# A two-layer transformer trunk: root of the sums without its own step, sums of exponentials in a ring, head scaling moved, and the last product in halves

## The chip, the cores and the metric

The kernel runs on one core of a Trainium2 chip. A core has TensorE (PE; PEld is its weight load), VectorE (DVE), ScalarE (ACT), GpSimd (POOL) and SyncE (SP), which only issues transfers here. The metric is the device time of one execution in microseconds. Matmuls write to PSUM, which has eight banks of 128x512 floats; the kernel gives four of them the tag "mm", two "s" and two "t".

## The reference, cut to what matters

The input is one sequence of 512 frames of width 1024, in float32. Two layers each compute, with `rms_norm(x, g) = x * rsqrt(mean(x*x) + EPS) * g`,

```python
y = mixer(rms_norm(x, attn_pre_g))
x = x + rms_norm(y, attn_post_g)
f = (silu(h @ w_gate) * (h @ w_up)) @ w_down      # h = rms_norm(x, ffn_pre_g)
x = x + rms_norm(f, ffn_post_g)
```

In layer 0 the mixer is a latent attention of 8 heads (q from a latent of 384, k and values from a latent of 256, a rotary part, a mask by chunks of 64 frames). In layer 1 it is an attention of 16 heads of width 64, with one key and value tensor projected from the residual stream, and a learned bias by distance. The feed-forward width is 2816.

## The kernel before, in words

Every matrix product is made three times: each operand is split into a high part (a cast on ScalarE, L144) and a low part (a subtraction on DVE, L145), and high·high, low·high and high·low are summed in PSUM (L361 to L363). The weights come in by SP's queue as `raw`, and their parts are called `whi` and `wlo`. The gate, up and down products of the feed-forward use seven block products in place of eight (`products`, L1524; `down`, L1280), for which DVE adds blocks of weights (L174).

Each engine has a queue of its own and executes it in order. The order in it is set when the program is built: a planner takes the instructions as they are written, with priorities that `first(n)` raises by n, and places them by its own estimate of when their inputs are ready. Thus a small edit can change the order at places that it doesn't mention.

**Attention** (`attention`, L546 and following) runs in slots, one per head and 128 queries. A slot computes the scores in a bank `sc` (L1069 to L1073 in layer 0, L1671 and L1672 in layer 1), their shifted values `p` and minimum `mn` on DVE (L527), exponentials with their row sums on ScalarE (L529), and two slots later the transposes `pt` (L541) and their split `pth`, `ptl`. When a head is complete, `pv` multiplies with the values (`b<-pth,va` in layer 0, L1679 and L1680 in layer 1). Between the slots, `weave` fills in the projections of later heads: q and k come out of `b` and are split into `qh`, `ql`, `kh`, `kl`; rotary parts are made by L971 to L973.

**The sums of exponentials** of a head stand in a tile `sums` of 128x32, memset to 1 on GpSimd for each. They are inverted on DVE (L1084, L1689), turned by a stream transpose (L503), written to memory by a transfer that GpSimd issues (`inv`) and read back, spread over the partitions, by two more (`rb`, L509). The head `of` is multiplied with `rb` (L1091 in layer 0, L1707 in layer 1), and then split into `oh` and `ol`. GpSimd's queue also holds the memsets of the bias tiles (L1603).

**Post-norms** sum squares of the projected bank by bank (`Sum.add`: Square on ScalarE, an addition on DVE, L439). `Sum.total` turns the sums on TensorE and reduces them on DVE (L452); `rstd` multiplies by 1/n and adds EPS on DVE (L463) and raises to the power −1/2 on GpSimd (L467); `spread` turns the result back over the partitions (L484). Between them TensorE works on.

**The last product.** `down` computes the 512x1024 result in quarters of two banks, each in seven steps; E6 is the last step, and its last group takes the weight tiles 3, 4 and 5. For each of its two banks (e is 0 or 1: the third and the fourth 128 rows) there follow: the last addition (L1347), the Square with its row sum (L1352), the gain (`yg`, L1467), the mean and EPS (`ssv`, L1389 and L1390), the root on GpSimd (L1393), and `plus_x` (L1491), which scales, adds the residual and sends the result out. `by_tokens`, called inside `products` of layer 1 three times for each pair of weight tiles, loads the residual stream back, turns it (L1196) and sends it to the output, to which the other rows' results are added.

Of the kernel before, what the change touches and what calls it, by code (L numbers as in the profile page):

```python
# [68 lines left out]
def trunk(ctx: ExitStack, tc: tile.TileContext, a, out):  # L69
# [353 lines left out]
    class Sum:  # L423


        def __init__(self, make=U):
            self.make, self.acc, self.begun = make, None, [False, False]

        def add(self, src, h=None):
# [4 lines left out]
            if not self.begun[h or 0]:  # L434
                ins = nc.scalar.activation(self.acc[:, c], src, AF.Square),
            else:
                q = self.make(name="sq")
                ins = (nc.scalar.activation(q[:, c], src, AF.Square),
                       V.tensor_tensor(self.acc[:, c], self.acc[:, c], q[:, c], op=OP.add))  # L439
            for i in ((0, 1) if h is None else (h,)):  # L440
                self.begun[i] = True
# [13 lines left out]
    def rstd(ss, n, eps=EPS):  # L455
        parts = ss if isinstance(ss, list) else [ss]
        m = sum(p.shape[1] for p in parts)
        v = small("v")[:, :m]
        w = m // len(parts)
        for i, p in enumerate(parts):  # L460
            o = v[:, i * w:(i + 1) * w]
            if eps is EPS:
                V.tensor_scalar(o, p, 1.0 / n, EPS, op0=OP.mult, op1=OP.add)  # L463
            else:
                V.scalar_tensor_tensor(o, p, 1.0 / n, eps[:, i * w:(i + 1) * w], op0=OP.mult, op1=OP.add)
        r = small("r")[:, :m]
        nc.gpsimd.tensor_tensor(r, v, mhalf[:, :m], op=OP.pow)  # L467
        return r

    def rstd_of_scaled(ss, n, r0):  # L470
# [4 lines left out]
        r = rstd(v, n)  # L475
# [19 lines left out]
    def sums_tile(i):  # L495
        t = pool[0].tile([P, 32], F32, tag="sums", name=f"sums_{i}", bufs=4)
        nc.gpsimd.memset(t, 1.0)
        return t

    def spread_dma(sums, i, m):  # L500

        t = pool[0].tile([P, 32], F32, tag="sumt", name=f"sumt_{i}", bufs=2)
        V.transpose(t, sums)  # L503
# [42 lines left out]
    def attention(n_heads, start, fill, first, units, after, pace=()):  # L546
# [18 lines left out]
        for i in range(slots + 3):  # L565
# [11 lines left out]
            if i >= 6 and i % NQT == 2:  # L577
                t = heads.pop((i - 6) // NQT)
                rest, far = t.pv(*t.pt)
                late.append((i + (NQT if far else 0), rest))  # L580
# [3 lines left out]
            if i % NQT == 3:  # L584
                scaled(i)
# [4 lines left out]
    class Post:  # L590
        def __init__(self, gain, make=U, eps=None, op=OP.add):

            self.gain, self.make, self.sum, self.y, self.r = gain, make, Sum(make), [], {}
            self.eps, self.op = eps, op

        def rstd(self, ss, h):
            return rstd(ss, D, EPS if self.eps is None else self.eps[:, 2 * h:2 * h + 2])
# [17 lines left out]
        def add_half(self, h, banks, rest, n1, n2, end=None):  # L615
# [7 lines left out]
            with behind(end and at):  # L623
                ss = self.sum.total(h, 200)
            with first(200):
                r = self.rstd(ss, h)
# [1200 lines left out]
```

## Time and profile before

| what | us |
|---|---|
| time, median of 3 runs (lowest, highest) | 1110.37 (1110.2, 1110.64) |
| the profiled execution's own time | 1110.27 |
| its span | 1108.5 |
| PE busy | 1094.3 |
| DVE busy | 936.8 |
| ACT busy | 678.3 |
| POOL busy | 91.7 |
| PE busy within 45 to 120 us (layer 0's attention) | 73.02 of 75.00 |
| PE busy within 560 to 700 us (layer 1's attention) | 138.21 of 140.00 |
| PE busy from 830 us to the end | 271.11 of 278.50 |

The granted clock of TensorE was 1.00 in each of these stretches. A row of a timeline gives the start, the duration, the engine, the line and operation with output and inputs, and in brackets how long the engine had been idle and whose end released it. Matmuls overlap: each lasts longer than the distance to the next start. A row of a list of waits gives the total, the number of times and the longest.

### The profile page before, as it was taken

To read this page: it belongs to the slowest core of one execution; us is meant where nothing else is said; L and a number is where in the kernel's file an instruction comes from. 1 tells how busy PE (TensorE), PEld (TensorE's weight loads), DVE (VectorE), ACT (ScalarE), POOL (GpSimd) and SP (SyncE) were. 2 spreads that over 40 slices of the span, in tenths; PEclk is the share of its full clock that TensorE was granted. 3 is DMA by queue.
4 is the path that set the end of the run, shared out by engine and by line. 5 is a ranking of instruction groups with operands and counts; after the bars stand their busy time and mean duration, and the time that the engine had idled before them with its cause. 6 is when DMAs were issued, how large, how long until landed. Compare 5 with 4: busy or idle time off the path is not lost.

```text
span 1108.5 us, 18978 instructions
## 1 busy us (share of the span) xinstructions
PE 1094.3 (99%) x6893; PEld 977.8 (88%) x6893; DVE 936.8 (85%) x1691; ACT 678.3 (61%) x1319; POOL 91.7 (8%) x158
## 2 busy tenths in 40 slices
PE   9999999999999999999999999999999999999997
PEld 6887889999999998888888788889999999998885
DVE  7778737999989989978868887758999999989977
ACT  6575737755555556668635676656755555556675
POOL 1211100000000001500000111000000000001402
PEclk9999999999999999999999999999999999999999
DMA  7443326323232357961556577635434444558913
GB/s 239 115 119 97 108 76 209 134 70 108 92 132 95 103 178 244 160 194 45 190 151 167 156 194 181 173 108 179 144 103 121 128 134 124 156 187 248 171 29 76
DMA packets 81421, 156.30 MB, mean 141 GB/s; under 512 B 26048, under 2 KB 27840, under 8 KB 81328
## 3 DMA queue, kind: packets, MB, share of 16 engines
q1 hardware_dynamic: 72448, 138.71, 40.5%
q0 software_dynamic: 8448, 15.95, 8.1%
q8 instruction: 54, 0.88, 0.3%
q10 hardware_dynamic: 432, 0.44, 0.1%
q14 instruction: 39, 0.32, 0.1%
HBM read 123.71 MB, written 10.88 MB: 121 GB/s over the span
## 4 chain that ended last, share of the span: by engine, by line
PE 85%; DVE 6%; DMA 4%; issue 2%; ACT 1%; SPq 1%; POOL 0%; DVEq 0%; POOLq 0%; ACTq 0%
PE al L1524 16%; PE b L361 10%; PE b L362 10%; PE b L363 10%; PE al L1280 8%; PE be L1524 8%; PE be L1280 5%; PE ga L1524 4%; PE de L1280 3%; PE ga L1280 3%; PE pt L541 2%; DVE wlo L145 2%; DVE raw L174 1%; DMA raw<-in_w_pair 1%; PE b L1680 1%
## 5 line engine op out<-in xcount | busy, mean ns | idle before, releaser
L144 ACT CAST whi<-raw 128x1024 fp32r<-128x1024 f32 (+3 forms) x224 | 225.0, 1006 | 200.6 <-PE al L1524 67.4
L145 DVE TENSOR_TENSOR wlo<-raw,whi 128x1024 fp32r<-128x1024 f32 (+3 forms) x224 | 260.1, 1164 | 43.3 <-ACT whi L144 41.9
L1524 PE MATMUL al<-th,whi 128*128 128x256 f32 x432 | 122.8, 285 | 0.2 <-DVE ut L1536 0.2
L1524 PE MATMUL al<-th,wlo 128*128 128x256 f32 x432 | 121.1, 281 | 0.3 <-DVE wlo L145 0.3
L1524 PE MATMUL al<-tl,whi 128*128 128x256 f32 x432 | 121.0, 280 | 0.0
L361 PE MATMUL b<-xh,whi 128*128 128x512 f32 (+1 forms) x298 | 114.8, 386 | 0.0
L363 PE MATMUL b<-xh,wlo 128*128 128x512 f32 (+1 forms) x298 | 110.0, 369 | 0.2 <-DVE wlo L145 0.2
L362 PE MATMUL b<-xl,whi 128*128 128x512 f32 (+1 forms) x298 | 109.8, 368 | 0.0
L174 DVE TENSOR_TENSOR raw<-raw,raw 128x1024 f32<-128x1024 f32 x72 | 86.9, 1218 | 1.1 <-DMA raw<-in_w_pair 0.8
L1524 PEld LDWEIGHTS al<-th,whi 128*128 128x128 f32 x432 | 81.3, 188 | 2.3 <-DVE ut L1536 0.6
L1524 PEld LDWEIGHTS al<-th,wlo 128*128 128x128 f32 x432 | 81.3, 188 | 0.6 <-DVE wlo L145 0.5
L1524 PEld LDWEIGHTS al<-tl,whi 128*128 128x128 f32 x432 | 81.4, 188 | 0.0
L529 ACT ACTIVATE p<-p,mn 128x128 f32<-128x128 f32 (+1 forms) x96 | 54.1, 563 | 37.6 <-DVE mn L527 37.2
L145 DVE TENSOR_TENSOR wlo<-wd,whi 128x512 fp32r<-128x512 f32 x86 | 56.4, 686 | 14.6 <-ACT whi L144 14.4
L145 DVE TENSOR_TENSOR ptl<-pt,pth 128x128 fp32r<-128x128 f32 (+1 forms) x96 | 46.4, 484 | 25.3 <-ACT pth L144 20.9
L363 PEld LDWEIGHTS b<-xh,wlo 128*128 128x128 f32 x298 | 56.2, 189 | 10.1 <-DVE wlo L145 0.6
L144 ACT CAST whi<-wd 128x512 fp32r<-128x512 f32 x86 | 49.8, 618 | 24.9 <-PE al L1280 10.7
L361 PEld LDWEIGHTS b<-xh,whi 128*128 128x128 f32 x298 | 56.5, 190 | 5.7
L362 PEld LDWEIGHTS b<-xl,whi 128*128 128x128 f32 x298 | 56.5, 190 | 5.5
L144 ACT CAST pth<-pt 128x128 fp32r<-128x128 f32 (+1 forms) x96 | 40.3, 421 | 28.3 <-PE pt L541 27.6
L245 POOL DMA_DIRECT2D wd<-in_w_down x22 | 19.5, 904 | 446.9 <-DVE raw L235 423.5
L1280 PE MATMUL al<-whi,pl 128*128 128x512 f32 x132 | 51.5, 390 | 0.0
(319 smaller groups left out, 3310.8 us busy)
## 6 DMA issues: line engine op xcount, KB each, us to landing
raw<-in_w_pair SPq DMA_DIRECT2D x72, 512.0 KB, 3.6
wd<-in_w_down SPq DMA_DIRECT2D x54, 256.0 KB, 5.9
raw<-in_w_o SPq DMA_DIRECT2D x16, 512.0 KB, 4.0
raw<-in_w_gu SPq DMA_DIRECT2D x16, 512.0 KB, 4.8
raw<-in_w_down SPq DMA_DIRECT2D x16, 512.0 KB, 4.3
raw<-in_w_qkb SPq DMA_DIRECT2D x16, 512.0 KB, 3.8
wd<-in_w_down POOLq DMA_DIRECT2D x22, 256.0 KB, 5.3
wd<-raw POOLq DMA_DIRECT2D x22, 256.0 KB, 4.2
```

The lines of the kernel that those rows point to most:

```text
L144: return (nc.scalar.copy(dst_hi, src), V.tensor_tensor(dst_lo, src, dst_hi.bitcast(F32), op=OP.subtract))
L145: V.tensor_tensor(dst_lo, src, dst_hi.bitcast(F32), op=OP.subtract))
L174: V.tensor_tensor(t, x, y, op=OP.add)
L245: nc.gpsimd.dma_start(p, self.src[0, e, :, c * S:c * S + S], accum_op=OP.add)
L361: nc.tensor.matmul(o, l[0], r[0], start=start, stop=False)
L362: nc.tensor.matmul(o, l[0], r[1], start=False, stop=False)
L363: last_mm[0] = nc.tensor.matmul(o, l[1], r[0], start=False, stop=stop)
L529: nc.scalar.activation(p[:, :n], p[:, :n], AF.Exp, bias=mn[:, :1], scale=-1.0, accum_out=self.sums[:, qt:qt + 1])
L541: nc.tensor.transpose(t[:, kt * P:(kt + 1) * P], p[:, kt * P:(kt + 1) * P], ident)
L1280: nc.tensor.matmul(to[e], l[c], r[d], start=j < 4 and k == 0 and n == 0, stop=k == NF // 2 - 1 and n == 2, skip_group_check=True)
L1524: nc.tensor.matmul(o, l[c], r[d], start=first_ and n == 0, stop=k == K2 - 1 and n == 2, skip_group_check=True)
L1680: nc.tensor.matmul(o[:, q_], vv, ptl[:, kt, q_], start=False, stop=kt == NQT - 1)
```

## The change

- `Sum` scales its squares by 1/1024 (the factor under the Square is 1024 to the power −1/2) and adds EPS/128 in its first addition, by one scalar_tensor_tensor. What `total` gives is then the mean plus EPS, and `rstd` is the power alone. Where the mean of fewer elements is wanted (the latents), the old way is kept, with the step written in `rstd_of_scaled`.
- The `sums` tiles become a ring of four (layer 0) and three (layer 1), memset once. The stream transpose of the sums has a priority of 60.
- A head's multiplication with `rb` and its split are written 7 slots behind its product with the values (for the last ones 5, or 1 as before), where it was 5. Whether one is due is asked in each slot, in layer 0 at its start and in layer 1 at its end; before, it was asked in layer 0 at the start of each, and in both layers at the end of every fourth.
- Two of the four value tiles of the first half take a bank of "s" instead of "mm".
- `by_tokens` isn't called in the first pair of `products`.
- In the last group of E6, bank e = 1 is computed in two halves of 256 columns, the first in its own bank, the second in a new one of tag "t", each with its own addition, Square, gain and `ssv` (`half`). What steps before the last group summed in the second half's columns is added to `y` ahead of it (`during`).

```diff
     class Sum:
-        def __init__(self, make=U):
-            self.make, self.acc, self.begun = make, None, [False, False]
+        def __init__(self, make=U, mean=True):
+            self.make, self.acc, self.begun, self.eps = make, None, [False, False], [mean, mean]
+            self.scale = D ** -0.5 if mean else 1.0
 ...
-            if not self.begun[h or 0]:
-                ins = nc.scalar.activation(self.acc[:, c], src, AF.Square),
+            t = self.acc[:, c]
+            both = (0, 1) if h is None else (h,)
+            if not self.begun[both[0]]:
+                ins = nc.scalar.activation(t, src, AF.Square, scale=self.scale),
             else:
                 q = self.make(name="sq")
-                ins = (nc.scalar.activation(q[:, c], src, AF.Square),
-                       V.tensor_tensor(self.acc[:, c], self.acc[:, c], q[:, c], op=OP.add))
+                ins = nc.scalar.activation(q[:, c], src, AF.Square, scale=self.scale),
+                if self.eps[both[0]]:
+                    ins += V.scalar_tensor_tensor(t, t, EPS / P, q[:, c], op0=OP.add, op1=OP.add),
+                    for i in both:
+                        self.eps[i] = False
+                else:
+                    ins += V.tensor_tensor(t, t, q[:, c], op=OP.add),
 ...
-    def rstd(ss, n, eps=EPS):
 ...
-                V.tensor_scalar(o, p, 1.0 / n, EPS, op0=OP.mult, op1=OP.add)
 ...
+    def rstd(v):
+        r = small("r")[:, :v.shape[1]]
+        nc.gpsimd.tensor_tensor(r, v, mhalf[:, :v.shape[1]], op=OP.pow)
         return r
 ...
-    def sums_tile(i):
-        t = pool[0].tile([P, 32], F32, tag="sums", name=f"sums_{i}", bufs=4)
-        nc.gpsimd.memset(t, 1.0)
-        return t
+    def sums_ring(n):
+        ring = [pool[0].tile([P, 32], F32, tag=f"sums{i}", name=name_("sums"), bufs=1) for i in range(n)]
+        for t in ring:
+            nc.gpsimd.memset(t, 1.0)
+        return ring
 ...
-        V.transpose(t, sums)
+        with first(60):
+            V.transpose(t, sums)
 ...
-                late.append((i + (NQT if far else 0), rest))
+                late.append((i + far, rest))
 ...
-            if i % NQT == 3:
+            if after:
                 scaled(i)
 ...
-            b = bank()
+            b = bank() if c or tt % 3 else bank("s")
 ...
-            return rest, far
+            return rest, (6 if h < H_A - 3 else 4) if far else 0
 ...
+                end = group[-1] == Down.TILES - 1
                 for e in range(2):
-                    for i, w, p in got:
 ...
+                    for o, cols in post.parts(j, e, to[e]) if end else ((to[e], ALL),):
+                        fresh = o is not to[e]
+                        for i, w, p in got:
 ...
+                        if cols is not ALL:
+                            post.half(o, cols)
+                        elif end:
+                            post.one(j, e, o)
 ...
+            if j == Down.E6 and i == 2:
+                t, c = self.y[0][3], HALF[1]
+                V.tensor_tensor(t[:, c], t[:, c], banks[1][:, c], op=OP.add)
 ...
+        def half(self, b, c):
+            t, v, q = self.y[0][3], self.v[:, 3:4], HALF.index(c)
+            with first(200):
+                V.tensor_tensor(t[:, c], t[:, c], b[:, c], op=OP.add)
+                sq = U(name="sq")
+                nc.scalar.activation(sq[:, c], t[:, c], AF.Square, accum_out=self.ends[:, q:q + 1])
+                if not q:
+                    self.yg = U(name="yg")
+                    V.scalar_tensor_tensor(v, self.ss[1][:, 3:4], 1.0 / D, self.eps[:, 3:4], op0=OP.mult, op1=OP.add)
+                V.tensor_tensor(self.yg[:, c], t[:, c], self.g[0][:, c], op=OP.mult)
+                self.summed = V.scalar_tensor_tensor(v, self.ends[:, q:q + 1], 1.0 / D, v, op0=OP.mult, op1=OP.add)
+                if q:
+                    self.y[0][3] = self.yg
+                    self.r[3] = small("r")[:, :1]
+                    nc.gpsimd.tensor_tensor(self.r[3], v, mhalf[:, :1], op=OP.pow)
 ...
                 if i == 2:
                     self.plus_x(1, 2, nc.sync)
+                    self.plus_x(0, 2, nc.scalar)
 ...
             with tc.issue_after(self.summed.ins):
-                self.plus_x(0, 2, nc.scalar)
                 self.plus_x(1, 3, nc.sync)
                 self.plus_x(0, 3, nc.scalar, nc.sync)
 ...
-                if aside is not None and j in (1, 3, 5):
+                if aside is not None and p and j in (1, 3, 5):
                     next(aside, None)
```

**How the order moves.** First, the post-norm of layer 1's attention, DVE's queue; `ss` is the reduced sum that the root needs, `wlo` the low part of a weight. Before:

```order
L452 TENSOR_REDUCE ss_8861<-tot_8858 128x2
L145 TENSOR_TENSOR wlo_9134<-raw_9049,whi_9133 128x1024
L463 TENSOR_SCALAR v_8863<-ss_8861 128x2
L439 TENSOR_TENSOR acc_8698<-acc_8698,sq_8893 128x256
L649 TENSOR_TENSOR y_8696<-y_8696,bc_8888 128x256
```

Now:

```order
L145 TENSOR_TENSOR wlo_9061<-raw_8923,whi_9060 128x1024
L460 TENSOR_REDUCE ss_8831<-tot_8828 128x2
L145 TENSOR_TENSOR wlo_9100<-raw_9017,whi_9099 128x1024
L447 TENSOR_TENSOR acc_8668<-acc_8668,sq_8861 128x256
L650 TENSOR_TENSOR y_8666<-y_8666,bc_8856 128x256
```

The step `v` behind the weight's part is gone; the reduction keeps its place.

Second, layer 0's attention where the fourth head's transposes are split, ScalarE's queue (`whi` is the cast of a weight, `qh` and `kh` those of q and k). Before:

```order
L144 CAST pth_1235<-pt_1320 128x4x128
L144 CAST qh_1241<-b_1170 128x512
L144 CAST whi_1551<-raw_1311 128x1024
L144 CAST kh_1243<-b_1247 128x512
L144 CAST qh_1327<-b_1288 128x512
```

Now:

```order
L144 CAST pth_1231<-pt_1314 128x4x128
L144 CAST whi_1536<-raw_1300 128x1024
L144 CAST qh_1237<-b_1161 128x512
L144 CAST kh_1239<-b_1243 128x512
L144 CAST qh_1321<-b_1277 128x512
```

The weight's cast has moved ahead of q's. On DVE its low part has moved ahead of `ql` in the same way, and on PE the first score matmul that reads `kh` has moved ahead of the product with the values.

Third, the end of DVE's queue. `be` are the banks of the last step, `last` the new one, `r` a root from GpSimd. Before:

```order
L1347 TENSOR_TENSOR y_12641<-y_12641,be_11914 128x512
L1467 TENSOR_TENSOR yg_12918<-y_12641,g_11944 128x512
L1390 SCALAR_TENSOR_TENSOR ssv_11909<-ss_1_11907,ssv_11909 128x1
L1491 SCALAR_TENSOR_TENSOR yg_12889<-yg_12889,r_12922,xt_12487 128x512
L1347 TENSOR_TENSOR y_12652<-y_12652,be_11915 128x512
L1467 TENSOR_TENSOR yg_12944<-y_12652,g_11944 128x512
L1390 SCALAR_TENSOR_TENSOR ssv_11909<-ss_1_11907,ssv_11909 128x1
L1491 SCALAR_TENSOR_TENSOR yg_12918<-yg_12918,r_12922,xt_12486 128x512
L1491 SCALAR_TENSOR_TENSOR yg_12894<-yg_12894,r_12948,xt_12491 128x512
```

Now:

```order
L1356 TENSOR_TENSOR y_12606<-y_12606,be_11879 128x512
L1482 TENSOR_TENSOR y_12617<-y_12617,be_11880 128x256
L1506 TENSOR_TENSOR yg_12884<-y_12606,g_11909 128x512
L1402 SCALAR_TENSOR_TENSOR ssv_11873<-ss_1_11871,ssv_11873 128x1
L1488 TENSOR_TENSOR yg_12913<-y_12617,g_11909 128x256
L1529 SCALAR_TENSOR_TENSOR yg_12854<-yg_12854,r_12888,xt_12452 128x512
L1529 SCALAR_TENSOR_TENSOR yg_12884<-yg_12884,r_12888,xt_12451 128x512
L1489 SCALAR_TENSOR_TENSOR ssv_11873<-ends,ssv_11873 128x1
L1482 TENSOR_TENSOR y_12617<-y_12617,last_12894 128x256
L1488 TENSOR_TENSOR yg_12913<-y_12617,g_11909 128x256
L1489 SCALAR_TENSOR_TENSOR ssv_11873<-ends,ssv_11873 128x1
L1529 SCALAR_TENSOR_TENSOR yg_12859<-yg_12859,r_12937,xt_12456 128x512
```

Both steps that scale the third row block now stand ahead of the last addition; before, one of them stood ahead of it and one behind. On PE, nine 256-column matmuls of `be_11880` now stand between the last but two and the last but one matmul of `be_11879`.

84 lines of the change are left out of this document (42 added, 42 removed).

## The prediction

> **What bounds the kernel now.** I read the page first: the busy times, and the chain of work that ended last.
>
> ```profile
> span 1108.5 us, 18978 instructions
> PE 1094.3 (99%) x6893; PEld 977.8 (88%) x6893; DVE 936.8 (85%) x1691; ACT 678.3 (61%) x1319; POOL 91.7 (8%) x158
> PE 85%; DVE 6%; DMA 4%; issue 2%; ACT 1%; SPq 1%; POOL 0%; DVEq 0%; POOLq 0%; ACTq 0%
> ```
>
> TensorE is busy in 1094.3 of 1108.5 us, and the chain is on it for 85%. No edit removes a matmul, so the time can change in two ways only: by the moments at which TensorE stands still, and by what follows its last matmul. The profiled execution took 1110.27 us, so 1.77 us lie around the span; the median of the runs is 1110.37, which is 0.10 above it. The list of TensorE's waits, next, is short. Its two largest rows:
>
> ```profile
> PE b L1680 <- DVE ptl L145: 1.5, 1, 1.5
> PE bc L484 <- POOL r L467: 0.9, 1, 0.9
> ```
>
> Then I went through the timeline of each wait, as below. The most that the change can win is some 5 us of 1110, so every term is a few tenths. From a gap between two starts I take off the pitch at which matmuls follow each other when nothing waits: 0.12 us with 256 columns (760.93 and 761.05 below), 0.23 with 512 (1100.51 and 1100.73 in the tail's rows).
>
> **The reciprocal root without its own step (L463).** The end of layer 1's attention projection, the timeline of DVE, GpSimd and PE, and one row of the same place in layer 0:
>
> ```profile
> 759.51 0.42 DVE L452 TENSOR_REDUCE ss<-tot 128x2 f32<-128x256 f32 x1
> 759.85 1.21 DVE L145 TENSOR_TENSOR wlo<-raw,whi 128x1024 fp32r<-128x1024 f32 x1
> 760.98 0.16 DVE L463 TENSOR_SCALAR v<-ss 128x2 f32<-128x2 f32 x1
> 761.29 0.90 POOL L467 TENSOR_TENSOR r<-v,mhalf 128x2 f32<-128x2 f32 x1 [51.56 <-ACT sq L438]
> 760.93 0.28 PE L361 MATMUL b<-oh,wh 128*128 128x256 f32 x1
> 761.05 0.28 PE L362 MATMUL b<-ol,wh 128*128 128x256 f32 x1
> 762.24 0.43 PE L484 MATMUL bc<-ident,r 128*128 128x128 f32 x2 [0.92 <-POOL r L467]
> 183.03 0.43 PE L484 MATMUL bc<-ident,r 128*128 128x128 f32 x2
> ```
>
> The step itself lasts 0.16 us; it costs more because a weight's low part (L145, 1.21) stands between the reduction and it. Without the step GpSimd reads the reduction, done at 759.93. It started 0.15 after its input was ready (761.29 against 761.14), so now at 760.08; 0.90 later is 760.98, and the spreading matmul starts 0.05 after that (762.24 against 762.19), at 761.03. TensorE gets there 0.24 earlier than before, since the order has it two matmuls of 0.12 sooner: at 761.17 − 0.24 = 760.93. The wait falls from 1.07 to 0.10: **−1.0 us**. In layer 0 the same weight step stands in the same place, and the gap was about 0.3: **−0.3**. The gain of EPS and mean in the sums is paid with one scalar_tensor_tensor where a tensor_tensor stood, under a tenth of a microsecond on DVE, hidden by matmuls. Bounds of both together: −1.4, and nothing, if another input is last.
>
> **Sums turned earlier, ring of tiles.** The first pair of heads in layer 1:
>
> ```profile
> 608.31 0.20 DVE L503 STREAM_TRANSPOSE sumt<-sums 128x32 f32<-128x32 f32 x1
> 611.52 0.14 POOL L1603 MEMSET bias<- 64x64 f32 x1 [1.58 <-DMA bias<-in_rel]
> 612.30 1.09 POOL L509 DMA_DIRECT2D rb<-inv  x2 [0.64 <-PE pt L541]
> 617.46 0.69 DVE L1707 TENSOR_TENSOR of<-of,rb 128x512 f32<-128x512 f32 x1 [1.73 <-DMA rb<-inv]
> 619.21 0.55 DVE L145 TENSOR_TENSOR ptl<-pt,pth 128x384 fp32r<-128x384 f32 x1
> 620.75 0.50 PE L1680 MATMUL b<-ptl,vb 128*128 128x512 f32 x1 [1.50 <-DVE ptl L145]
> ```
>
> DVE waits 1.73 us for the reciprocals that travel through memory, ptl comes late, and TensorE stands 1.5 (1.65 by the starts). In the new order the transpose stands three rows sooner on DVE, some 0.8 us. But GpSimd's queue still holds the bias memset, which waits for its own load until 611.52, ahead of the second transfer: that one can start at about 611.7 instead of 612.30, so 0.6 is likely, and a transfer that starts ahead of its neighbours may also land faster: half of the remaining 1.05 on top. **−1.1** (0 to −1.65). The multiplication keeps its place among DVE's rows; only the split of the scaled head moves, and nothing reads it soon. The other pairs, and the first layer:
>
> ```profile
> 692.02 0.49 PE L1679 MATMUL b<-pth,vb 128*128 128x512 f32 x1 [0.24 <-ACT pth L144]
> 74.63 0.20 DVE L503 STREAM_TRANSPOSE sumt<-sums 128x32 f32<-128x32 f32 x1
> 82.83 0.69 DVE L1091 TENSOR_TENSOR of<-of,rb 128x512 f32<-128x512 f32 x1 [1.05 <-DMA rb<-inv]
> 86.66 0.50 PE L362 MATMUL b<-ptl,va 128*128 128x512 f32 x1 [0.59 <-DVE ptl L145]
> 97.63 0.50 PE L361 MATMUL b<-ckh,whi 128*128 128x512 f32 x1 [0.22 <-DVE ra L971]
> 105.04 0.63 PE L541 MATMUL pt<-ident,p 128*128 128x128 f32 x4
> 105.70 0.59 ACT L144 CAST pth<-pt 128x512 fp32r<-128x512 f32 x1 [0.54 <-PE pt L541]
> 106.19 0.59 ACT L144 CAST qh<-b 128x512 fp32r<-128x512 f32 x1
> 106.86 1.04 ACT L144 CAST whi<-raw 128x1024 fp32r<-128x1024 f32 x1
> 106.93 0.68 DVE L145 TENSOR_TENSOR ql<-b,qh 128x512 fp32r<-128x512 f32 x1
> 107.67 0.51 PE L361 MATMUL b<-pth,va 128*128 128x512 f32 x1 [0.61 <-DVE ql L145]
> ```
>
> At 692.02 DVE had been late by an earlier wait of the same kind; transpose and sums are a row earlier: **−0.4** (0 to −0.5). In layer 0 the first head's sums are turned right behind their reciprocal, over 3 us before 74.63, so the 1.05 us at 82.83 goes, and with it the stand at 86.66 (starts 85.67 and 86.66, less 0.23): **−0.75**. Scaling 7 slots behind instead of 5 takes the split `ol` (some 0.68, like `ql` at 106.93) out of DVE's way ahead of the rotary steps, and the matmul at 97.63 finds its bank free: its 0.22 and the slower start behind it, **−0.4**.
>
> **The price of the new order in layer 0.** Behind the fourth transpose at 105.04, ScalarE had cast q, then the weight; now the weight is first, and on DVE its low part stands ahead of `ql`. Count from the transposes' start t. ScalarE's first cast begins at t + 0.66 and the next 0.49 later (105.70, 106.19); the weight's cast ends at t + 2.2, q and k at t + 2.7 and t + 3.2. DVE's low part of the weight (1.13 from 759.85 to 760.98 above) then ends at t + 3.35, `ql` at t + 4.0. Before, `ql` was done at 107.61, t + 2.57, and TensorE was there at t + 1.85. The new order has the first score matmul, which needs k, only four matmuls of 512 behind the transposes, at t + 1.3, and the product with the values two short ones later. That product needs the bank that `ql` empties, so it starts at about t + 4.1: a stand of some 2.6 instead of 0.75. **+1.9**, between 0 (the cast of the weight gets done ahead of the transposes) and +2.4. Layer 0's attention thus gives −0.75 − 0.4 + 1.9 = **+0.75**. The value tiles that now take their banks from the scores' pair change no wait that I found: nothing, and up to ±0.3.
>
> **Products.** With the by-tokens work out of pair 0, its transposes stand in later pairs:
>
> ```profile
> 820.69 0.70 DVE L1196 STREAM_TRANSPOSE xt<-x 128x512 f32<-128x512 f32 x1
> 823.70 0.38 PE L1524 MATMUL al<-th,wlo 128*128 128x256 f32 x1 [0.33 <-DVE wlo L145]
> ```
>
> 0.70 us less ahead of the weight's low part covers the wait: **−0.4** (0 to −0.5). The later pairs already carried one such transpose each without a wait this long.
>
> **The tail.** The end of the last group on all engines:
>
> ```profile
> 1100.51 0.39 PE L1280 MATMUL be<-wlo,ph 128*128 128x512 f32 x1
> 1100.73 0.39 PE L1280 MATMUL be<-whi,pl 128*128 128x512 f32 x1
> 1101.16 0.69 DVE L1347 TENSOR_TENSOR y<-y,be 128x512 f32<-128x512 f32 x1 [0.36 <-PE be L1280]
> 1101.88 0.63 ACT L1352 ACTIVATE sq<-y 128x512 f32<-128x512 f32 x1 [2.72 <-DVE y L1347]
> 1102.64 0.16 DVE L1390 SCALAR_TENSOR_TENSOR ssv<-ss,ssv 128x1 f32<-128x1 f32 x1
> 1102.88 1.00 POOL L1393 TENSOR_TENSOR r<-ssv,mhalf 128x1 f32<-128x1 f32 x1 [2.87 <-DVE ssv L1390]
> 1103.91 1.54 DVE L1491 SCALAR_TENSOR_TENSOR yg<-yg,r,xt 128x512 f32<-128x512 f32 x3 [0.45 <-POOL r L1393]
> 1099.44 0.57 POOL L1393 TENSOR_TENSOR r<-ssv,mhalf 128x1 f32<-128x1 f32 x1 [3.43 <-DVE ssv L1390]
> ```
>
> Thirty matmuls of 256 columns take 3.5 us where fifteen of 512 took 3.4: +0.1, and TensorE ends at about 1101.2 as before. What was meant is plain: the last add and square have 256 columns, 0.42 instead of 0.69 (the reduction above has that size) and some 0.2 less on ScalarE: −0.5. But DVE's order puts two `plus_x` steps of the third row block, which wait for GpSimd's root, **ahead** of the last half's add. Nine matmuls of the other half now run before the first bank is done, so that is done 1.0 later, at 1098.7; then follow on DVE an add (0.7), a half add (0.4), a gain (0.65), the sum `ssv` at about 1100.5. GpSimd starts 0.24 later and takes 0.57 to 1.00 (both rows above): 1101.3 to 1101.75. Two `plus_x` and a small sum bring DVE to 1102.8 to 1103.3, long after TensorE has ended. Only then come the half add (0.4), the square (0.55), the sum (0.15), the wait for GpSimd again (0.65 to 1.1) and the last three steps (1.54): DVE ends at 1106.25 to 1107.1 instead of 1105.45, so +0.8 to +1.65: **+1.2**; −0.5 is kept as the other bound. The Trainium skill (PSUM — Partial Sum Buffer, Engine vs sequencer instructions) says that VectorE's queue is strictly first in, first out; by that rule the half add can't pass the two steps, and the trace agrees: DVE's 1101.16 to 1103.91 run in the order written.
>
> **Sum.** −1.0 − 0.3 − 1.1 − 0.4 + 0.75 − 0.4 + 1.2 = −1.25. The profiled execution would take 1110.27 − 1.25 = 1109.02; with the 0.10 that the median lies above, 1109.1.
>
> **The rivals.** *A, the tail as meant*: GpSimd's first root comes so early that the two `plus_x` steps are done when TensorE ends. Then −0.5 stands for +1.2, and the result is 1107.4. For it: GpSimd took only 0.57 the last time but one. Against it: even with that, `ssv` at 1100.5 gives 1101.3, and 1.5 us of steps follow. The Trainium skill (Perfetto Trace Analysis, Optimizing Scalar/DVE Operations) says that where Vector isn't saturated but causes bubbles, breaking up instructions may complete the work sooner; by that rule the result is this rival's. No row before the change shows a half. *B, the early turn wins nothing*: the second transfer is held by its neighbours, not by the transpose; then the 1.1, 0.4 and 0.75 are lost, 1111.4. For it: GpSimd's memset, and that DVE had its reciprocals only 5 us after 612.30; against it: the head at 82.83 has 3 us to spare. *C, slower*: a weight cast ahead of q and k also decides in the next two heads of layer 0, where the order again puts one before k; each costs 1.9, 3.8 together, 1112.9. It decides where k is asked for less than about 3.2 us after the transposes. Against it: other heads give TensorE value products between. *D*: both the tail and the stand at 105 cost nothing: 1109.1 − 1.7 − 1.9 = 1105.5.
>
> **Chances.** Forecast 0.48, its own range 1107.8 to 1110.4; A 0.22, B 0.17, C 0.08, D 0.05. A measurement of this kernel tells a change from none at about 0.2%, 2.2 us: faster is below 1108.15, slower above 1112.6. Faster: all of A and D and a quarter of the forecast, 0.39. Slower: C, 0.08. Within: 0.53. The range goes from 1106.8, which leaves out D and the better part of A, to 1111.4, which takes in B.
>
> **What would show it.** Right: GpSimd's root starts directly behind the reduction near 760, with no TensorE wait over 0.2 there; DVE's wait for `rb` in the first pair of layer 1 falls below 1.2, and that of layer 0 is gone; a TensorE stand of 2 us or more near 105; the last 256-column add runs over a microsecond after TensorE's last matmul. Wrong: DVE idle at that add until TensorE ends, which is A; TensorE's sum of waits in layer 0's attention lower by over a microsecond, which leads to D; or waits for `kh` in several heads, C.

## The result, and the profile after

The changed kernel takes 1118.69 us (median of 4 runs, 1116.1 to 1119.83), the kernel before, run beside it, 1110.44 (1110.2 to 1110.64): a ratio of 1.0071, interval 1.0051 to 1.0091. It is slower by some 8 us; 1109.1 was forecast, with 1111.4 as the upper end. The profiled execution took 1117.65 us, 7.4 more than the one before. The head of its page, and the largest rows of TensorE's waits (total, times, longest; the 1.2 us of the warm-up at the start, in both kernels, left out):

```profile
span 1115.9 us, 18985 instructions
PE 1096.5 (98%) x6908; PEld 980.7 (88%) x6908; DVE 938.9 (84%) x1687; ACT 678.1 (61%) x1321; POOL 92.2 (8%) x149
PE b L1719 <- DVE ptl L145: 3.5, 4, 1.3
PE sc L1071 <- ACT kh L144: 2.4, 2, 1.9
PE b L361 <- DVE va L145: 1.5, 1, 1.5
PE bc L483 <- POOL r L465: 0.6, 1, 0.6
```

Two rows are new (`kh`, `va`), one has grown (`ptl`, 1.5 before), and one has shrunk by 0.3 instead of going (`bc`, 0.9 before). To place the loss I took, for each two neighbouring matmuls, the distance of their starts less the pitch of the first one's width (0.06, 0.118, 0.176 and 0.23 us for 128, 256, 384 and 512 columns, 0.11 for a transpose of 128), and summed it by stretches. This is what TensorE loses there, to waits and to a lower clock. Some small loss is everywhere. In microseconds, with five experiments that are told below (`only_late`, `late_h1`, `only_vals`, `only_rt` and `only_root`):

| stretch | before | before, again | changed | late alone | late, not head 0 | banks alone | turn alone | root alone |
|---|---|---|---|---|---|---|---|---|
| 0–45 | 2.8 | 2.7 | 2.0 | 4.0 | 3.1 | 3.8 | 3.6 | 3.0 |
| 45–70 | 1.1 | 1.1 | **4.2** | 1.0 | 1.1 | **4.3** | 1.1 | 1.1 |
| 70–95 | 2.0 | 1.7 | 1.0 | 1.9 | 1.4 | 1.4 | 1.2 | 1.7 |
| 95–125 | 3.8 | 3.8 | **6.8** | **5.6** | 3.7 | 3.6 | 4.0 | 3.8 |
| 125–235 | 2.0 | 1.9 | 1.5 | 2.0 | 1.5 | 2.0 | 1.6 | 1.0 |
| 235–560 | 1.9 | 2.1 | 1.8 | 0.8 | 1.8 | 2.3 | 2.0 | 1.5 |
| 560–705 | 5.5 | 8.0 | 7.7 | 9.7 | 6.4 | 4.6 | 9.2 | 8.2 |
| 705–760 | 1.5 | 1.6 | 1.5 | 2.0 | 1.3 | 1.5 | 1.5 | 1.4 |
| 760–835 | 1.9 | 2.1 | 0.9 | 1.8 | 1.8 | 1.9 | 1.8 | 1.4 |
| 835–end | 1.5 | 1.9 | 3.0 | 1.6 | 1.7 | 2.0 | 1.6 | 1.5 |

From the first column to the third this is +6.7; of the rest of the 7.4, 0.6 lies behind TensorE's last matmul (7.4 us to the span's end before, 7.9 now). The stretches that lost are 45–70, 95–125, 560–705 and the end.

**95 to 125 us.** The predicted stand is there. PE, ACT and DVE around it, then windows of two microseconds (length; busy times of PE, PEld, DVE, ACT and POOL with their instructions; granted clock, DMA share, GB/s):

```profile
107.69 1.05 ACT L144 CAST whi<-raw 128x1024 fp32r<-128x1024 f32 x1
109.12 0.59 ACT L144 CAST kh<-b 128x512 fp32r<-128x512 f32 x1
107.49 0.39 PE L363 MATMUL b<-ckh,wlo 128*128 128x512 f32 x1
109.76 0.68 PE L1071 MATMUL sc<-kh,qh 128*128 128x128 f32 x2 [1.88 <-ACT kh L144]
110.69 0.80 PE L361 MATMUL b<-pth,va 128*128 128x512 f32 x1 [0.24 <-DVE ql L145]
107.00:109.00 2.00, 0.88 (x4) 0.38 (x2) 1.55 (x4) 1.88 (x3) 0.73 (x1) 1.00 0.59 123
109.00:111.00 2.00, 0.99 (x3) 0.70 (x4) 2.00 (x3) 1.68 (x4) 0.63 (x2) 0.73 0.63 158
111.00:113.00 2.00, 2.00 (x8) 1.72 (x8) 1.42 (x3) 0.00 (x0) 0.42 (x1) 0.50 0.85 252
113.00:115.00 2.00, 2.00 (x9) 2.00 (x9) 1.28 (x5) 1.39 (x4) 0.00 (x0) 0.50 0.93 256
117.00:119.00 2.00, 2.00 (x14) 1.69 (x13) 0.60 (x2) 1.21 (x5) 0.00 (x0) 1.00 0.00 0
```

TensorE stands 2.04 us for `kh` (107.49 to 109.76, less 0.23) and then 0.64 for `ql`, 2.7 together, where the forecast had 2.6. What it did not have is the column of the clock: behind the stand it is 0.50 until about 116.7 us, with 8 or 9 matmuls in two microseconds where 14 run at 1.00. By starts, 106 to 111 us loses 3.2 (before: 1.8), and 111 to 118 loses 2.8 (before: 0.4).

**45 to 70 us.** DVE near 57 us, with the matmul that waits; the changed kernel, then the one before:

```profile
55.96 0.68 DVE L973 TENSOR_TENSOR ra<-b,sin 128x512 f32<-128x512 f32 x1
56.56 0.68 DVE L974 TENSOR_TENSOR rb<-b,cos 128x512 f32<-128x512 f32 x1
57.15 0.81 DVE L145 TENSOR_TENSOR wlo<-raw,whi 128x640 fp32r<-128x640 f32 x1
57.89 0.68 DVE L145 TENSOR_TENSOR va<-b,va 128x512 fp32r<-128x512 f32 x1
58.62 0.50 PE L361 MATMUL b<-whi,ckh 128*128 128x512 f32 x1 [1.50 <-DVE va L145]
```

```profile
55.27 0.82 DVE L145 TENSOR_TENSOR wlo<-raw,whi 128x640 fp32r<-128x640 f32 x1 [0.57 <-ACT whi L144]
56.76 0.68 DVE L145 TENSOR_TENSOR va<-b,va 128x512 fp32r<-128x512 f32 x1
57.36 0.68 DVE L971 TENSOR_TENSOR ra<-b,sin 128x512 f32<-128x512 f32 x1
57.49 0.50 PE L361 MATMUL b<-whi,ckh 128*128 128x512 f32 x1
```

The value product of a later token tile needs the bank that DVE's `va` empties. Before, `va` ran first; now two rotary products and a weight's low part, 2 us together, stand ahead of it. That order came with the banks, as the experiments show. By the starts this stand is 1.65 us (0.28 before); a second one of 0.71, in which the scores wait for `kh` at 66.71, is new too, and the rest of the 3.1 us lost here is in smaller pieces.

### The profile page after: what moved, and what is told of

It is laid out like the page before. It is cut to its first block, busy times and chain, and to the rows that moved or that the text cites. A ratio compares the mean times of both kernels' runs of the same rounds, so it can differ in the third digit from the quotient of the medians.

```text
span 1115.9 us, 18985 instructions
## 1 busy us (share of the span) xinstructions
PE 1096.5 (98%) x6908; PEld 980.7 (88%) x6908; DVE 938.9 (84%) x1687; ACT 678.1 (61%) x1321; POOL 92.2 (8%) x149
## 4 chain that ended last, share of the span: by engine, by line
PE 83%; DVE 7%; DMA 5%; issue 2%; ACT 1%; SPq 1%; POOL 1%; DVEq 0%; POOLq 0%; ACTq 0%
PE al L1562 17%; PE b L361 10%; PE b L362 9%; PE b L363 9%; PE be L1562 8%; PE al L1287 8%; PE be L1287 5%; PE ga L1562 4%; PE de L1287 3%; PE ga L1287 3%; PE pt L542 2%; DVE wlo L145 2%; PE b L1719 1%; DMA rb<-inv 1%; PE b L1718 1%
```

## The experiments

Each ratio is against the kernel before on the same chip, with its interval. First, two parts taken out of the changed kernel, each with its lines as they were.

```diff
-            return rest, (6 if h < H_A - 3 else 4) if far else 0
+            return rest, NQT if far else 0                     # no_late, and the same in layer 1
-            if after:
+            if i % NQT == 3:                                   # no_late
-            b = bank() if c or tt % 3 else bank("s")
+            b = bank()                                         # no_vals
```

> The changed kernel with one part undone: a head's scaling is written 5 slots behind its values again, in both layers. Theory 1 (the later scaling reorders layer 0's attention, and the stand of 2.7 us at 107 us also takes TensorE's clock to half for some 5 us): the stand falls under 1 us, the granted clock stays at 1.00 from 45 to 120 us, layer 1's waits for rb fall from 4.1 to about 3, and the time is 1111 to 1113. Rival 1 (the other parts cost it: the halves, the bank of the values, the by-tokens work): 1117 or more. Both leave the stand of 1.65 us at 57 us, since the value tiles' banks alone give that order too.

> The changed kernel with all value tiles in the banks mm again. Theory 1: DVE's order near 57 us stays as in the changed kernel, since the later scaling gives it too, so the stand of 1.65 us stays; time 1117.5 to 1119.5. Rival 2 (the banks taken from s make that wait): the stand goes, 1115.5 to 1117.

Without the later scaling 1.0045 (1.0029 to 1.0061), without the banks 1.0043 (1.0025 to 1.0061), against 1.0071. Each is worth some 3 us, a difference of two ratios that is itself uncertain by about 3 us; each part alone, below, costs 2.0 and 2.8 us. Without the scaling the clock stays at 1.00 from 45 to 120 us and the stand at 107 is 0.78; without the banks 45 to 70 loses 1.1, and the slow clock stays. Two expectations missed. `no_late` took 1116.25 us, between its two ranges, and layer 1's waits for `rb` rose from 4.1 to 5.3 us instead of falling to 3. And theory 1 of `no_vals` kept the stand near 57 us, since the later scaling would give that order too; its rival came true, the order comes with the banks alone, as the table's 45–70 row shows.

Then the later scaling alone on the kernel before, and a test of its second half: does a stand of this length halve the clock by itself? `gaps` computes nothing of the reference; it alternates 66 to 78 matmuls of 512 columns with stands of eight lengths, five times, with no transfers in between.

```diff
+        for k in LENGTHS:                       # DVE additions that the next matmul waits for
+            for j in range(m): nc.tensor.matmul(b[1] if j else b[0], h[:, :P], h, ...)
+            for j in range(k): nc.vector.tensor_tensor(y[:, :256], y[:, :256], b[1][:, :256], op=OP.add)
```

> The kernel before with one part added: the scaling 7 slots behind. Theory 1: the stands at 57 (1.5 us) and 107 us (2.5 us) with half the clock behind the second, and more waits for rb in layer 1; 1115 to 1119. Rival 1: 1111.5 or less.

> Only stretches of 66 to 78 matmuls of 512 columns, with stands of about 1.5 to 4.2 us between them, five times each length; nothing of the reference is computed. Theory 1 (a stand alone lowers the clock): behind stands shorter than some length between 2 and 3 us the matmuls start every 0.23 us as before, behind longer ones every 0.43 us for some 3 to 7 us. Rival 3 (the half clock comes from the transfers of 250 GB/s that run at that moment in the changed kernel): 0.23 us behind all of them.

The later scaling alone gives 1.0018 (1.0007 to 1.0030), 1113.51 us, between the ranges of the two expectations; it has the stand at 107 us and not the one at 57. In `gaps`, of stands of 1.12 and 1.58 us none is followed by slow matmuls (10 stands), of 2.04 three of 5, of 2.49 all 5, of 2.95 four of 5, of 3.40 and more all 14. The slow stretch costs 1.3 to 2.9 us, mostly 1.7. Windows of ten microseconds around a stand of 1.58, two of 2.04 and one of 2.49:

```profile
36.00:46.00 10.00, 8.58 (x38) 6.77 (x37) 1.84 (x5) 0.00 (x0) 0.00 (x0) 1.00 0.00 0
57.00:67.00 10.00, 8.12 (x29) 6.25 (x28) 2.26 (x6) 0.00 (x0) 0.00 (x0) 0.83 0.01 2
222.00:232.00 10.00, 8.12 (x36) 6.36 (x35) 2.26 (x6) 0.00 (x0) 0.00 (x0) 1.00 0.00 0
76.00:86.00 10.00, 7.67 (x27) 5.81 (x26) 2.68 (x7) 0.00 (x0) 0.00 (x0) 0.83 0.00 0
```

So transfers are not needed for it, and it begins between 1.6 and 2.5 us. What decides in between is where the stand falls. In `gaps` the granted clock changes only on a grid of 3.41 us (at 59.81, 63.23, 80.29, 83.70 us and so on), and behind a stand it is 0.50 for one or two whole steps of it, as in these two:

```profile
59.82:63.22 3.40, 3.40 (x9) 2.63 (x10) 0.42 (x2) 0.00 (x0) 0.00 (x0) 0.50 0.03 5
124.68:128.08 3.40, 3.40 (x10) 2.63 (x9) 0.00 (x0) 0.00 (x0) 0.00 (x0) 0.50 0.00 0
```

The 13 stands with at most 1.62 us in any one step are followed by no slow matmul, among them two of 2.04 and one of 2.95 that the border of a step divides; the 26 with 1.97 us or more in one step all are. In the kernels the border lies near 2 us as well: `no_late` has a stand of 2.06 us in layer 1, 2.03 of it in one step, without slow matmuls. The grid lies differently in each execution (the clock first rises 6.69 us into one profile of the kernel before and 5.41 into the other). So a given stand can cost the clock in one run and not in the next; the mean granted clock fits this, 0.994 to 0.995 in three of the changed kernel's four runs and 0.999 in the fastest (1116.1 us). The Trainium skill (TensorE: Matmul & The Clock Gate, Why this matters for your kernels) advises to leave no gap over about 3 us between bursts of matmuls. Here the measurement decides: the limit is lower, about 2 us within one step of the grid.

Next, what is left without the two parts; the kernel before again, for its profile; four small parts (root, ring, turn, by-tokens) alone; and the halves taken out.

> The changed kernel without the late scaling and without the values' new banks. Theory: these two cost some 3 us each and are all that made the changed kernel slower; what is left is the gain at the roots and turns (-1.8 us) and the tail (+0.6): ratio 0.999, between 0.998 and 1.001, the clock at 1.00 from 45 to 120 us, and about 1 us lost from 45 to 70. Rival: another part (the tail in halves, or the longer waits of layer 1) costs as much: 1.003 or over.

> The kernel before once more, to have its profile on the chip on which the other experiments ran. In layer 1 (560 to 705 us) the changed kernel and its first three variants lost 7.7 to 9.7 us on TensorE's start-to-start times, the kernel before 5.3 in its first profile. Theory: the change itself lengthens the waits there (layer 1's values, the place of the by-tokens product): this profile shows 5.3 +- 0.5 us again, and the three waits for the value tile ptl of a pair's second half stay at 2.9 us together. Rival: they vary from one execution or one chip to another: over 7 us here too. Ratio 1.000 in either case.

> The kernel before with four parts of the change alone: no separate root step, the early turn of the sums with its ring of tiles, the mean and epsilon made with the squares, and the products and by-tokens order; without the late scaling, the values' new banks and the last group in halves. Theory: the terms of the prediction that are left are -1.0 and -0.3 for the root step, -0.4 and -0.75 for the early turn (the first pair's -1.1 was not seen in the changed kernel), which with +0.6 for layer 1's longer waits is about -1.8 us, ratio 0.998. Rival: the waits won there come back behind the next one: ratio 1.000.

> The changed kernel with the last group whole, as before. Theory: the halves cost the 0.6 us by which the span's end moved away from TensorE's last matmul (8.0 us against 7.4): 0.6 us under the changed kernel, ratio 1.0065 to the one before. Rival: the halves help as they are meant to, and the longer tail of the one profile comes from elsewhere: ratio 1.008 or over.

Measured: no_late_vals 1.0021 (1.0011 to 1.0032), between its two expectations, so these two are not all; before_again 1.0002 (0.9993 to 1.0011), with 8.0 us lost in layer 1 against 5.5 in the first profile; keep4 1.0011 (1.0001 to 1.0021), a loss where 0.998 was expected; no_halves 1.0061 (1.0047 to 1.0075), which can't be told from the changed kernel's 1.0071. The rival on layer 1 holds in part: the same program loses 2.5 us more or less there. Its timeline and DVE's waits from 560 to 705 us show why:

```profile
607.94 1.23 DVE L309 TENSOR_TENSOR raw<-raw,gains 128x1024 f32<-128x1024 f32 x1 [1.51 <-DMA raw<-in_w_qkb]
DVE raw L309 <- DMA raw<-in_w_qkb: 10.0, 4, 3.4
DVE of L1707 <- DMA rb<-inv: 3.8, 4, 1.4
```

A weight that came in time in the first profile is awaited 1.5 us in this one, and the score tiles queue behind it on DVE (1.5 us more lost by TensorE near 610); the second pair's `rb`, not awaited in the first profile, is awaited 1.15 (1.1 lost near 640). A stretch of layer 1 must not be compared between two single profiles.

Then each small part alone, five rounds each:

```diff
+        with first(60):                          # only_rt, with the rings; turn_l1: first(0 if i < H_A else 60)
             V.transpose(t, sums)
-                if aside is not None and j in (1, 3, 5):
+                if aside is not None and p and j in (1, 3, 5):      # only_aside
```

`only_root` is the change's edit of `Sum` and `rstd`, `only_halves` its edit of the last group. `best1` is only_root with the rings and `first(60 if i < H_A else 0)`; `late_h1` is only_late with `6 if 0 < h < H_A - 3 else 4`.

> The kernel before with the root step alone (scale in the squares, epsilon in the adds). The four small parts together came out 1.2 us slower (ratio 1.0011, 1.0001 to 1.0021) though their profile shows the waits at the roots and at layer 0's sums shorter. Theory A: the root step wins what its waits show, 0.3 to 0.5 us near 183 and 1.0 near 761, and costs nothing elsewhere: ratio 0.9988. Theory B: what it wins is lost again in layer 1's start (560 to 705 us), whose waits for late weight transfers and value tiles took 5.5 us in one profile of the kernel before and 8.0 in another: 1.000, with over 7 us there.

> The kernel before with the turned sums alone (their priority and the ring of tiles). Theory A: 0.4 us are won from 70 to 95 us and nothing is lost: ratio 0.9997. Theory B: the earlier turn puts the pair's three small transfers ahead of other work in layer 1 and costs some 2 us there: 1.001 to 1.002, with over 7 us lost from 560 to 705 us.

> The kernel before with the by-tokens product moved past layer 1's first pair of products alone. Theory A: it costs nothing (I had forecast -0.4 us): ratio 0.9996 to 1.000. Theory B: this is the part that makes the four small ones slower, by waits for the up-projection's tile ut behind 835 us (0.5 us more there in the changed kernels): 1.0005 to 1.002.

> The kernel before with the last group in halves alone. Theory A: two applications of the factor stand ahead of the last half's add, the end moves 0.6 us away from TensorE's last matmul, and the halves' matmuls add 0.1: ratio 1.0005. Theory B: the halves are worth what they cost: 1.000. Theory C: they cost more than the tail shows, as the step from the four small parts (1.0011) to the kernel with the halves but without late scaling and banks (1.0021) would have it: 1.001.

> The kernel before with the ring of tiles and the priority of the turn in layer 1 alone. Theory A: the turned sums cost in layer 1: with the earlier turn VectorE's product by the spread sums stands one or two score groups earlier in its queue at the third pair and waits there for its transfer, and the three transfers meet more traffic (they landed 4.5 us after their issue with the earlier turn, 4.1 without): 1.0015 to 1.002, over 8.5 us lost from 560 to 705 us. Theory B: what only_rt showed was chance, or layer 0's: 1.000.

> The kernel before with the root step, the ring of tiles and the early turn in layer 0 alone. Theory A: the root step's gain (0.9989) and layer 0's wait of 0.4 to 0.5 us near 86 us add up: 0.9985, 1109.0 us, which would beat both kernels. Theory B: what the ring of tiles or layer 0's turn wins is lost again in layer 1, which waits for its transfers whatever comes before: 0.9995 or over.

> The kernel before with the later scaling for all heads but the first, whose scaling stays at 4 slots: with that ScalarE's queue at 107 us is as before (query and key casts ahead of the weight cast). Theory A: the stand at 107 us and the halved clock behind it are all that the later scaling costs: ratio 0.999 to 1.0003, the clock at 1.00 from 95 to 125 us and 3.8 us lost there. Theory B: it costs in layer 1 too (9.7 us were lost from 560 to 705 us with the later scaling alone, against 5.5 and 8.0 before): 1.001 or over.

| part alone | ratio | interval |
|---|---|---|
| root step | 0.9989 | 0.9979 to 0.9999 |
| turned sums, both layers | 1.0016 | 1.0004 to 1.0028 |
| the same, layer 1 alone | 1.0013 | 1.0002 to 1.0025 |
| root step and layer 0's turn | 0.9996 | 0.9986 to 1.0005 |
| by-tokens moved | 0.9997 | 0.9984 to 1.0010 |
| halves | 1.0001 | 0.9990 to 1.0011 |
| later scaling, all but the first head | 0.9998 | 0.9988 to 1.0008 |

The root step wins, by an interval that only just leaves out 1. The early turn loses, and in layer 1; layer 0's adds nothing to the root step that can be told. The later scaling costs nothing once the first head keeps its 4 slots: the clock stays at 1.00 from 95 to 125 us, and the new order at 107 was its whole price as far as this can be measured. Its windows from 95 to 125 us, of the scaling alone and without the first head:

```profile
95.00:125.00 30.00, 27.60 (x149) 23.75 (x148) 23.65 (x55) 18.75 (x46) 5.73 (x11) 0.94 0.40 116
95.00:125.00 30.00, 28.86 (x162) 24.07 (x161) 24.66 (x59) 20.65 (x49) 5.72 (x11) 1.00 0.47 135
```

Why the early turn loses: the timeline of only_rt at the first and the third pair, and then the third pair's product of the kernel before.

```profile
608.59 0.20 DVE L505 STREAM_TRANSPOSE sumt<-sums 128x32 f32<-128x32 f32 x1
612.44 1.09 POOL L511 DMA_DIRECT2D rb<-inv  x2 [0.89 <-DMA inv<-sumt]
618.37 0.69 DVE L1742 TENSOR_TENSOR of<-of,rb 128x512 f32<-128x512 f32 x1 [2.05 <-DMA rb<-inv]
658.40 0.69 DVE L1742 TENSOR_TENSOR of<-of,rb 128x512 f32<-128x512 f32 x1 [0.85 <-DMA rb<-inv]
659.01 0.68 DVE L145 TENSOR_TENSOR ptl<-pt,pth 128x512 fp32r<-128x512 f32 x1
659.75 0.50 PE L1715 MATMUL b<-ptl,vb 128*128 128x512 f32 x1 [0.64 <-DVE ptl L145]
```

```profile
655.29 0.69 DVE L145 TENSOR_TENSOR ptl<-pt,pth 128x512 fp32r<-128x512 f32 x1
656.48 0.69 DVE L1707 TENSOR_TENSOR of<-of,rb 128x512 f32<-128x512 f32 x1
```

At the first pair the turn still comes behind a weight for which DVE waits, so the transfers start no sooner, and land no sooner. At the third pair the planner, presumably because it now expects `rb` sooner, has put the product one score tile earlier: ahead of `ptl`. The transfer isn't there, and `ptl` waits behind it. TensorE loses 0.4 to 1.9 us at this place in all eight kernels with layer 1's early turn, and nothing that shows (over 0.15 us) in the eleven without it. Whether this is the whole of the part's 1.4 to 1.8 us is not shown, since the stretch varies by 2.5 us from one profile to the next.

Last, the banks alone, the bank "s" for the first token tile alone (`bank() if c or tt else bank("s")`), and the root step with late_h1, to which the runs pointed:

> The kernel before with the values' banks alone. Theory A: they cost what the windows of the kernels that have them show, 4.2 to 4.5 us lost from 45 to 70 us against 1.1: +3.2 us, ratio 1.0029. Theory B: as the turned sums did in part, the loss is made up by shorter waits further on: 1.001 or less, with 4.2 us still lost from 45 to 70 us.

> The kernel before with an s bank for the values of the first token tile alone, not for the first and the last. VectorE's queue near 57 us is then ra, rb, va, ra, va, wlo in place of ra, rb, wlo, va. Theory A: the stand of 1.65 us near 57 us comes from the weight's rest (1.2 us of VectorE) ahead of the first values: it falls to 0.5 us or less, 1 to 2 us are lost from 45 to 70 us, ratio 1.000 to 1.001. Theory B: it comes from the two rotary products or from the bank itself: the stand stays over 1 us, ratio 1.002 or over.

> The kernel before with the root step and the later scaling for all heads but the first. Theory A: the root step's 0.9989 and the later scaling's 0.9998 add up: 0.9987, which beats both kernels with an interval under 1. Theory B: the gain before layer 1 is lost again in the waits there, as it was with the root step and layer 0's turn together (0.9996): 0.9996 or over.

The banks alone cost 1.0025 (1.0015 to 1.0035), with 4.3 us lost from 45 to 70. `vals_0` comes out at 1.0039 (1.0025 to 1.0053): the weight's part is behind the values, yet a stand of 0.98 remains where 1.65 was, for the two rotary products, and another of 1.9 appears:

```profile
58.35 0.50 PE L361 MATMUL b<-whi,ckh 128*128 128x512 f32 x1 [0.82 <-DVE va L145]
```

The second is for `kh`, at 66.89, and the clock behind it is 0.50 from 68 to 70 us. So neither expectation covers it: both kinds of work ahead of `va` count, and both uses of the scores' bank that were tried reorder the stretch to its harm (5.2 us lost from 45 to 70 here). `best2` gives 0.9989 (0.9979 to 0.9998), as the root step does alone. Either is 0.1%, some 1.2 us, faster than the kernel before; the later scaling adds nothing that can be told.

## Why the prediction was wrong, step by step

Three steps failed: the banks' term, put at nothing, cost 3 us; the clock behind the new stand had no term and cost 2.4; and the turned sums, forecast to win 1.5 us in layer 1, lost 1.4 there (1.0013).

**Bound and method.** The bound "the most that the change can win is some 5 us" holds, but nothing in the sum bounded what it can lose. "The time can change in two ways only", by TensorE's stands and by the tail, left out a third: matmuls that run at half the clock. Between the two waits that the prediction calls the largest the list has a third, 1.2 us of the warm-up matmuls at the start, which is the same in both kernels.

**Root step, −1.0 and −0.3: its size was wrong in layer 1.** The root starts where the forecast had it, 0.15 us behind the reduction (765.78 + 0.42, 766.35), but takes 1.56 us instead of 0.90. The changed kernel:

```profile
765.78 0.42 DVE L460 TENSOR_REDUCE ss<-tot 128x2 f32<-128x256 f32 x1
766.12 1.22 DVE L145 TENSOR_TENSOR wlo<-raw,whi 128x1024 fp32r<-128x1024 f32 x1
766.35 1.56 POOL L465 TENSOR_TENSOR r<-ss,mhalf 128x2 f32<-128x2 f32 x1 [50.81 <-DVE ss L460]
767.97 0.43 PE L483 MATMUL bc<-ident,r 128*128 128x128 f32 x2 [0.64 <-POOL r L465]
```

The weight's part, which stood ahead of the root before, now runs beside it, and the root ends 0.57 after it (767.91 and 767.34), about what a root takes by itself. Layer 0 shows the same; before, with VectorE idle beside the root, and then changed:

```profile
182.26 0.72 POOL L467 TENSOR_TENSOR r<-v,mhalf 128x2 f32<-128x2 f32 x1 [52.35 <-DVE v L463]
```

```profile
185.65 1.61 POOL L465 TENSOR_TENSOR r<-ss,mhalf 128x2 f32<-128x2 f32 x1 [50.91 <-DVE ss L460]
```

So moving it ahead of that step saved its own wait, not the weight's. The Trainium skill (SBUF — State Buffer, SBUF: two separate sides) says that VectorE with two SBUF inputs and GpSimd share a pair of ports as an exclusive lock, and that the one who starts later waits for the whole instruction; the trace agrees, with 1.56 and 1.61 us against 0.72. The wait fell from 0.92 to 0.64, and layer 0's small gap went as said. The part as a whole still gave about 1.2 us (0.9989), near the forecast's 1.3; since these two rows account for only 0.6 of it, that agreement is in part luck.

**Turned sums, −1.1, −0.4 and −0.75: the sign was wrong in layer 1.** In the first pair the rows of `only_rt` fit rival B: the second transfer is issued when the first has landed, and lands 5.9 us later (612.44 to 618.37; 5.2 before), while the DMA engines are busy for 0.74 of the time. That its neighbours hold it was not tested by itself. The changed kernel's wait for `rb` there is 1.51, not under 1.2. The sentence "The multiplication keeps its place among DVE's rows" was checked at the first pair only, and fails at the third. Layer 0's wait did go (70–95: 1.0 against 1.7 and 2.0).

**Later scaling, −0.4 and +1.9.** Both were right: the stand is 2.7 us. Missing was the term behind it, 2.4 us of half clock in the changed kernel (2.8 less 0.4) and 1.6 in the scaling alone. No row of the kernel before has a stand over 1.7 us, and its clock never showed this; the forecast took the clock as given. Rival C, the one that said slower, needed a stand of this size at the next two heads as well. TensorE's list has two waits for `kh`, 1.88 us here and 0.55 near 67 us, so C did not come true.

**Values' banks, "nothing, and up to ±0.3".** This is the largest loss of any part, +3.1 (alone 1.0025, 2.8 us). I had looked for new waits on banks, not for a new order of DVE near 57 us, where the product's bank is emptied late.

**Products, −0.4.** The wait near 823 did go, with some 0.6 us between 760 and 835 for the part alone (1.35 there, against 1.9 and 2.1), but 0.5 to 0.8 come back behind 835 (2.4 against 1.5 and 1.9; one stand of 1.0 near 990 is new). By itself it gives 0.9997.

**Tail, +1.2: mechanism right, size half.** The changed kernel:

```profile
1107.33 0.68 POOL L1405 TENSOR_TENSOR r<-ssv,mhalf 128x1 f32<-128x1 f32 x1 [4.63 <-DVE ssv L1402]
1107.63 0.28 PE L1287 MATMUL last<-whi,pl 128*128 128x256 f32 x1
1108.04 1.41 DVE L1529 SCALAR_TENSOR_TENSOR yg<-yg,r,xt 128x512 f32<-128x512 f32 x2 [0.47 <-POOL r L1405]
1109.45 0.41 DVE L1482 TENSOR_TENSOR y<-y,last 128x256 f32<-128x256 f32 x1
1111.26 1.54 DVE L1529 SCALAR_TENSOR_TENSOR yg<-yg,r,xt 128x512 f32<-128x512 f32 x3 [0.67 <-POOL r L1493]
```

The two `plus_x` steps stand between TensorE's end and the last half's add, 1.5 us late (1107.91 and 1109.45). DVE ends 4.9 us behind TensorE where it was 4.3: +0.6, since both roots took 0.55 to 0.68 and the upper bound had 1.00. By itself the part makes no difference that can be told (1.0001), and the two steps run where rival A, the tail as meant, has them done: A falls. The Trainium skill's rule on breaking up instructions (Perfetto Trace Analysis, Optimizing Scalar/DVE Operations), which spoke for that rival, gained nothing here.

**The sum.** The parts alone add up to −1.1 + 1.6 + 1.8 + 2.5 − 0.3 + 0.1 = +4.6 thousandths, 5.1 us, against 7.9 for the whole. The intervals of seven ratios allow that difference (2.8 ± 3.8 us), and the runs don't settle whether the parts also harm each other; without the scaling and the banks 2.3 us are left, where the other four parts alone add up to 0.3 (a difference of 2.0 ± 2.8).

## What to carry to other kernels

Where a planner sets the order, compare it on every engine over the whole program, also for a part that "changes no wait": the three costly parts all worked through rows that their diff doesn't name. When a step goes, look at what ran beside it: an instruction that becomes ready earlier may then meet the work that it used to follow. Price a stand of TensorE by its length and by the clock behind it, and try the parts one by one, since one that wins may come in with three that lose.

## What the runs showed that I had not expected

- A stand of 2.04 us halves TensorE's clock in 3 of 5 cases and one of 2.49 in 5 of 5, for 6 to 13 matmuls at 0.43 us in place of 0.23; what decides is whether some 2 us of it fall into one step of a grid of 3.41 us. In the scaling alone it struck a second time, behind a stand of 1.9 us in layer 1 (window 645 to 647 us of only_late; clock in the column behind POOL):

```profile
645.00:647.00 2.00, 2.00 (x6) 1.58 (x6) 0.88 (x2) 0.78 (x2) 0.00 (x0) 0.50 0.55 188
```

- A root of two columns on GpSimd takes 0.72 us by itself and 1.56 to 1.61 beside a VectorE instruction of 1.2 us with two inputs.
- Transfers set how long layer 1's start takes: two executions of one program differ by 2.5 us there, by the waits for a weight (1.5 us) and for the second pair's `rb` (1.15 us) that only one of them has.
